# The low-query term of the attention logits, over 64 rows or over 128 with zeros

## The chip, the core and the metric

The kernel runs on one core of a Trainium2 chip. Its engines are TensorE (PE in the profile, with PEld for the loads of its stationary operand), VectorE (DVE), ScalarE (ACT), GpSimd (POOL) and SyncE (SP), whose queue issues the loads. The metric is the device time of one execution in microseconds, lower is better. Three runs of the kernel before took 865.79, 867.05 and 867.57 us; the median is 867.05.

## The reference

One layer of a hybrid decoder trunk over 512 tokens of width 1024, all in float32. A combined projection of the normalized input feeds three token mixers (a gated causal convolution, differential attention, causal pooling), whose outputs are gated, summed and projected; a squared-ReLU MLP and a gated embedding follow, each added to the residual. The change is in the attention, which has 4 heads with two softmax maps each over 64 dimensions:

```
q = q * (ATTN_HD ** -0.5)
for start in range(0, S, Q_BLOCK):                       # blocks of 128 queries
    qb, kb, vb = q[:, start:end], k[:, :end], v[:, :end]
    logits = jnp.einsum("bqhmd,bkhmd->bhmqk", qb, kb)    # m: the two maps, d: 64
    logits = jnp.where(dist >= 0, logits + bias, -1e30)
    probs = jax.nn.softmax(logits, axis=-1)
    attn = probs[:, :, 0] - lam * probs[:, :, 1]
    outs.append(jnp.einsum("bhqk,bkhe->bqhe", attn, vb))
```

## The kernel before

*Products in three terms.* A float32 operand is split into a rounded high part and the exact rest, both of a type (float32r) that TensorE multiplies quickly. A product is the sum of three matmuls, high with high, high with low and low with high; the helper at L153 to L155 issues them. Weights come in 144 chunks of 128 x 1024 through three raw slots; ScalarE rounds each chunk (L89) and VectorE subtracts (L93), into three pairs of slots (wh, wl).

*The order of work.* In its first half the kernel runs through the list ORDER: projections of conv, q and k, v and pool tiles, then gates and output products. Between the matmuls of these projections a clock of credit lets background streams (convolution, attention, pooling) issue their steps. The instructions are then ordered on each engine by the framework's scheduler, and each engine runs its own queue in that order. Heads 0 to 3 of the attention have their q and k projected at four places in the list, and `evac_qk` brings each out of PSUM.

*q and k of a head.* The 128 partitions of a projected tile hold the 64 dimensions of map 0 (LO) and of map 1 (HI). For each map m, `own` names its half and `other` the opposite one. Tile q[m] holds the high part of q twice, in both halves; k[m] holds the high part of k in `own` and the low part in `other`. One matmul of q[m] and k[m] over 128 rows (L460) is thus the sum of two terms, high q with high k and high q with low k. The third term, low q with high k, is a matmul over the 64 rows of `own` (L462). One tile `ql` serves both maps, each with its half. Both matmuls add into one PSUM bank.

*The logits.* For each head and each of 4 query blocks there are two maps, so 32 matmuls of L460 and 32 of L462, over 256, 256, 384 and 512 key columns. VectorE adds the bias and takes the maximum (L466), ScalarE does the exponential (L472), the two maps are combined, transposed on TensorE against an identity (L493), split, and multiplied by v. GpSimd clears the parts of the transposed tiles that stay zero (L498), issues the stores of an early projection (L364) and takes the powers of the norms (L202). The tiles q, ql and k come from one pool of 10 slots, five for a head.

Of the kernel before, what the change touches and what calls it, by code (L numbers as in the profile page):

```python
# [13 lines left out]

# the work of the first half in order, by the letters of the table
ORDER = [dict(A="conv", Q="qk", V="v", P="pool", p="pool out", a="attention out", c="conv gates")[c]
         for c in "QAVPAAQQQppppcAaaaaccc"]
# shares of TensorE's time given to the background work during projections and gates
RATE_IN, RATE_GATE = 0.6, 0.907
# of the steps of background work, how many are taken from the first queue for one from the second  # L20
TURNS = 2
# steps to wait for the sums of a norm: a head's, the last head's, LayerNorm's
NORM_LAG, WAIT_SUB, WAIT_LN = 10, 4, 8
# start: tiles of x loaded before the second chunk; chunks split before x is normalized; normalized
# tiles of x before the next chunks; products that bring up the array's clock
X_BEFORE_W1, W_EARLY, XN_BEFORE_W3, XN_BEFORE_W4, N_WARM = 3, 2, 2, 7, 8
# products of a half before the other half's sums, and before they are spread; chunks split after that
PACE_SUM, PACE_SPREAD, W_AHEAD = 8, 15, 3
# output tiles multiplied side by side before those by halves
N_SIDE = 3  # L30
# slots: raw chunks, split chunks, activations, logits, tiles of norms, q and k
N_RAW, N_SPLIT, N_ACT, N_LOGIT, N_NORM, N_QK = 3, 3, 32, 6, 3, 10
TCARGS = dict(schedule_with_timeline_sim=True)
# [11 lines left out]

# columns of the packed small parameters
G_PRE_MIX, G_POST_MIX, G_PRE_MLP, G_POST_MLP = 0, 8, 16, 24
# [9 lines left out]
class Weights:  # L57
    """Streams the packed weight chunks in order: a load and a split of each
    chunk into its rounded high part and the exact rest."""

# [50 lines left out]
def block_kernel(ctx: ExitStack, tc: tile.TileContext, xT, pT, wts, pool_w, par, rel_bias, onehot, out):  # L111
# [15 lines left out]

    # tiles that wait for a long chain have slots of their own: slots of a tag are
    # given out in order, so they would hold up all that comes after them
    BUFS = {"a": N_ACT, "lg": N_LOGIT, "bias": 2, "norm": N_NORM}  # L130
# [15 lines left out]
    def mul_split(h, l, src, scale=1.0):  # L146
        """h + l = src * scale, h rounded to the fast product's operand."""
        nc.scalar.activation(out=h, in_=src, func=AF.Copy, scale=scale)  # L148
        nc.vector.scalar_tensor_tensor(out=l, in0=src, scalar=scale, in1=h.bitcast(F32),  # L149
                                       op0=ALU.mult, op1=ALU.subtract)  # L150
# [5 lines left out]

# [1 line left out]
    start = ExitStack()  # L158
# [28 lines left out]
    nc.vector.memset(neghalf, -0.5)  # L187
    # products whose result nobody reads, so that the array's clock is up when the data comes
    warm = bank("at")
# [5 lines left out]

# [1 line left out]
    def rstd_from(ssq, inv_n, n, name):  # L197
        """[P, n] sums -> (sum * inv_n + eps) ** -0.5"""
        c = small(n, name + "c")
        nc.vector.tensor_scalar(out=c, in0=ssq, scalar1=inv_n, scalar2=EPS, op0=ALU.mult, op1=ALU.add)  # L200
        r = small(n, name + "r")
        nc.gpsimd.tensor_tensor(out=r, in0=c, in1=neghalf[:, 0:n], op=ALU.pow)  # L202
        return r

    def rstd_steps(sq, lo, n, inv_n, got, tag="at"):
        """column sums of sq[:, lo:lo+128n] to rstd, the same on every partition, in PSUM: a step
        for the sums and one that spreads them and hands them to got"""
        b = bank(tag)
        for j in range(n):
            nc.tensor.matmul(out=b[:, j:j + 1], lhsT=sq[:, lo + j * P:lo + (j + 1) * P], rhs=ones_col,  # L210
                             start=True, stop=True)
        r = rstd_from(b[:, 0:n], inv_n, n, "pe")
        yield
        for j in range(n):
            nc.tensor.matmul(out=b[:, j * P:(j + 1) * P], lhsT=r[:, j:j + 1].to_broadcast([P, P]),  # L215
                             rhs=ident, start=True, stop=True)
        got(b[:, 0:n * P])
# [16 lines left out]

    # ---- background streams: steps for DVE between the products, each step
    # yielding its cost in us, or None when it can't go on yet ----
    class Stream:
# [3 lines left out]
        def step(self):  # L241
            """one step; its cost, or None when the stream is blocked or over"""
            try:
                return next(self.gen)
            except StopIteration:
                self.over = True
                return None
# [41 lines left out]

# [1 line left out]
    LEFT, RIGHT = slice(0, 512), slice(512, 1024)  # L291
# [73 lines left out]

# [1 line left out]
    lam_t = cp.tile([P, 8], F32, name="lam_t")  # L367
# [11 lines left out]

    # sigmoid(z) = (1 + tanh(z / 2)) / 2, so that one table serves exp and the gates;  # L380
    # the factor 1/2 goes where a scale is applied anyway
    nc.vector.tensor_scalar(out=pcol(DW_W, 4 * CW), in0=pcol(DW_W, 4 * CW), scalar1=0.5, scalar2=None, op0=ALU.mult)
# [9 lines left out]
    nc.sync.dma_start(out=rel_d, in_=rel_r)  # L392
    # row r of a head's bias is its row of distances moved by r
    rep_d = dr.tile([NH, P, 640], F32, name="rep_d")
# [3 lines left out]

# [1 line left out]
    def project(n, evac, side_by_side=False):  # L400
        """n output tiles of the combined projection"""
        bs = []
# [17 lines left out]
    def evac_qk(bs):  # L420
        """q and k of a head's two maps, stacked so that a product over 128 rows holds two of the
        three terms: high q twice against high and low k; and low q where the high k lies"""
        qb, kb = bs
        ql = act_tile("ql", F32R, "qk", qkp)
        q, k = ([act_tile(n, F32R, "qk", qkp) for _ in range(2)] for n in "qk")
        for m, (own, other) in enumerate(((LO, HI), (HI, LO))):
            nc.scalar.activation(out=q[m][own], in_=qb[own], func=AF.Copy, scale=ATT_SCALE)
            nc.scalar.activation(out=q[m][other], in_=qb[own], func=AF.Copy, scale=ATT_SCALE)
            nc.vector.scalar_tensor_tensor(out=ql[own], in0=qb[own], scalar=ATT_SCALE, in1=q[m][own].bitcast(F32),
                                           op0=ALU.mult, op1=ALU.subtract)  # L430
            nc.scalar.copy(out=k[m][own], in_=kb[own])
            nc.vector.tensor_tensor(out=k[m][other], in0=kb[own], in1=k[m][own].bitcast(F32), op=ALU.subtract)
        return q, ql, k
# [15 lines left out]
    def attention():  # L449
        state = {}  # L450

        def logits(i):
# [6 lines left out]
            for m in range(2):  # L459
                nc.tensor.matmul(out=lg[m][:, 0:nn], lhsT=q[m][:, cols], rhs=k[m][:, 0:nn], start=True, stop=False)  # L460
            for m, own in enumerate((LO, HI)):
                nc.tensor.matmul(out=lg[m][:, 0:nn], lhsT=ql[own, cols], rhs=k[m][own, 0:nn], start=False, stop=True)  # L462
            mx, sm = small(2, "mx"), small(2, "sm")
# [23 lines left out]
        def transpose(i):  # L487
            # keys of all blocks up to this pair of query blocks on the partitions
            qb = i % 4
# [196 lines left out]

# [1 line left out]
    merged = [None] * KT  # L688
# [78 lines left out]

    # ---- output projection; its last tiles by token halves, so that the norm
    # of one half runs while the other half is multiplied ----
    x_t = []  # L770
# [13 lines left out]
    class Paced:  # L784
        """the steps of a norm, set between the products of the other half"""

# [14 lines left out]
    def split_output(src, evac, done):  # L801
        """8 output tiles of a product over 8 kt: some side by side, the others by halves."""
        W.limit = chunk[0] + KT + 3
# [38 lines left out]
    def residual_half(hf, src, ssum, rB, xs, use):  # L842
        """xs += src * rstd of the half, and what uses the sum"""
        sl = HALVES[hf]
# [18 lines left out]

# [1 line left out]
    def side_by_side_halves(src, done):  # L865
# [67 lines left out]

# [1 line left out]
    proj = []  # L935
# [36 lines left out]
def _layout(inp):  # L972
# [7 lines left out]
    def tiles(w):  # L980
        """[K, M] -> [M/128][128, K/128, 128]"""
        k, m = w.shape
        return w.reshape(k // P, P, m // P, P).transpose(2, 1, 0, 3)
# [88 lines left out]
```

## Time and profile before

| what | value |
|---|---|
| time, median of 3 runs | 867.05 us (865.79 to 867.57) |
| span of the profiled execution (no other time of it is given) | 864.5 us |
| TensorE matmul busy, instructions | 848.3 us (98%), 4202 |
| VectorE busy | 512.3 us (59%) |
| ScalarE busy | 352.5 us (41%) |
| GpSimd busy | 50.4 us (6%) |
| chain of work that ended last, share of TensorE | 86% |
| mean granted TensorE clock | 0.993 |

The span is the time from the first instruction to the last. Busy time of TensorE counts each matmul from its start to its modelled end, and one starts before the other has ended, so two matmuls in a row are compared by their starts. In a timeline row the numbers are the start, the time the row covers, the engine, the line, the operation, output and inputs by the program's names, rows*columns of the array that the operation uses, the shape it streams, and the count of instructions that the row merges; brackets give idle time ahead of it and what ended that.

### The profile page before, as it was taken

The numbers are of one execution on the slowest core, as the hardware profiler recorded it, in microseconds if no ns is written. First come the engines' busy times: TensorE is split into PE (matmuls) and PEld (weight loads), VectorE is DVE, ScalarE is ACT, GpSimd is POOL, SyncE is SP. The second block draws the span as 40 slices with busy tenths as digits, with TensorE's granted clock in tenths as the row PEclk, the third lists the DMA queues.
The fourth block names the chain that finished last, engine by engine and source line by source line (L and its number), as shares of the span: only waits on it lengthen the run. The fifth ranks groups of instructions, "written<-read, shape, count | busy, mean of one in ns | idle before, by whom it ended". The sixth has DMA issues, their size and how long they took to land.

```text
span 864.5 us, 10723 instructions
## 1 busy us (share of the span) xinstructions
PE 848.3 (98%) x4202; PEld 707.9 (82%) x4202; DVE 512.3 (59%) x803; ACT 352.5 (41%) x568; POOL 50.4 (6%) x85
## 2 busy tenths in 40 slices
PE   9979999999999999999999999999999999999998
PEld 6767888777778888888999778888888888889987
DVE  5749659965559996658368453344344434425682
ACT  6625435464443323553454354342124313425341
POOL 2100000010000000000033100000000000000420
PEclk9989999999999999999999999999999999999999
DMA  8353222121122222255201614222222222212311
GB/s 296 122 194 114 106 98 98 68 91 54 69 74 74 96 99 96 76 191 204 91 27 53 204 49 146 98 98 97 99 98 98 97 90 88 99 65 75 122 50 74
DMA packets 28127, 89.38 MB, mean 103 GB/s; under 512 B 3272, under 2 KB 3656, under 8 KB 28076
## 3 DMA queue, kind: packets, MB, share of 16 engines
q1 hardware_dynamic: 27260, 86.32, 28.6%
q0 software_dynamic: 816, 2.37, 0.7%
q8 instruction: 33, 0.54, 0.2%
q14 instruction: 18, 0.15, 0.1%
HBM read 84.47 MB, written 5.52 MB: 104 GB/s over the span
## 4 chain that ended last, share of the span: by engine, by line
PE 86%; DVE 5%; DMA 4%; issue 3%; ACT 1%; POOL 1%; SPq 0%; DVEq 0%; ACTq 0%; POOLq 0%
PE mm L153 19%; PE mm L155 19%; PE mm L154 19%; PE at L153 8%; PE at L154 8%; PE at L155 8%; DMA raw<-in_wts_dram 2%; DVE f L850 1%; PE at L462 1%; PE at L215 1%; POOL x L851 1%; PE at L210 1%; DVE mix L850 1%; PE at L460 1%; PE at L493 1%
## 5 line engine op out<-in xcount | busy, mean ns | idle before, releaser
L89 ACT CAST wh<-raw 128x1024 fp32r<-128x1024 f32 (+1 forms) x144 | 148.6, 1038 | 334.5 <-PE mm L154 151.0
L93 DVE TENSOR_TENSOR wl<-raw,wh 128x1024 fp32r<-128x1024 f32 (+1 forms) x144 | 173.4, 1209 | 104.6 <-ACT wh L89 104.3
L155 PE MATMUL mm<-xnh,wl 128*128 128x512 f32 x352 | 138.6, 394 | 0.1
L153 PE MATMUL mm<-xnh,wh 128*128 128x512 f32 x352 | 137.9, 394 | 0.0
L154 PE MATMUL mm<-xnl,wh 128*128 128x512 f32 x352 | 137.8, 392 | 0.0
L582 DVE SCALAR_TENSOR_TENSOR acc<-u,par_sb,acc 128x512 f32<-128x512 f32 x116 | 82.2, 748 | 0.1
L153 PEld LDWEIGHTS mm<-xnh,wh 128*128 128x128 f32 x352 | 66.1, 188 | 15.7 <-issue 1.0
L155 PEld LDWEIGHTS mm<-xnh,wl 128*128 128x128 f32 x352 | 66.1, 188 | 15.0 <-issue 0.8
L154 PEld LDWEIGHTS mm<-xnl,wh 128*128 128x128 f32 x352 | 66.1, 188 | 13.8 <-DVE xnl L149 0.4
L153 PE MATMUL mm<-sh,wh 128*128 128x512 f32 (+1 forms) x152 | 54.4, 358 | 0.0
L154 PE MATMUL mm<-sl,wh 128*128 128x512 f32 (+1 forms) x152 | 54.2, 357 | 0.0
L155 PE MATMUL mm<-sh,wl 128*128 128x512 f32 (+1 forms) x152 | 54.2, 356 | 0.0
L154 PE MATMUL at<-xgl,wh 128*128 128x512 f32 (+1 forms) x144 | 52.8, 366 | 1.2 <-DVE xgl L149 1.2
L153 PE MATMUL at<-sh,wh 128*128 128x512 f32 (+1 forms) x144 | 53.4, 371 | 0.3 <-ACT sh L148 0.3
L154 PE MATMUL at<-sl,wh 128*128 128x512 f32 (+1 forms) x144 | 53.1, 369 | 0.2 <-DVE sl L149 0.2
L155 PE MATMUL at<-sh,wl 128*128 128x512 f32 (+1 forms) x144 | 52.9, 367 | 0.0
L153 PE MATMUL at<-xgh,wh 128*128 128x512 f32 (+1 forms) x144 | 52.9, 367 | 0.0
L153 PE MATMUL mm<-xgh,wh 128*128 128x512 f32 (+1 forms) x144 | 52.7, 366 | 0.0
L155 PE MATMUL at<-xgh,wl 128*128 128x512 f32 (+1 forms) x144 | 52.7, 366 | 0.0
L154 PE MATMUL mm<-xgl,wh 128*128 128x512 f32 (+1 forms) x144 | 52.6, 365 | 0.0
L155 PE MATMUL mm<-xgh,wl 128*128 128x512 f32 (+1 forms) x144 | 52.6, 365 | 0.0
L202 POOL TENSOR_TENSOR per<-pec,neghalf 128x4 f32<-128x4 f32 (+1 forms) x10 | 10.5, 1052 | 533.2 <-DVE pec L200 533.2
(247 smaller groups left out, 1583.3 us busy)
## 6 DMA issues: line engine op xcount, KB each, us to landing
raw<-in_wts_dram SPq DMA_DIRECT2D x140, 512.0 KB, 3.2
x<-in_xT_dram SPq DMA_DIRECT2D x16, 256.0 KB, 5.9
proj_d<-proj POOLq DMA_DIRECT2D x8, 256.0 KB, 3.9
proj<-proj_d SPq DMA_DIRECT2D x8, 256.0 KB, 3.7
out_dram<-pg SPq DMA_DIRECT2D x7, 256.0 KB, 2.0
rep_d<-rel_d SPq DMA_DIRECT2D x1, 1280.0 KB
raw<-in_wts_dram SPq DMA_DIRECT2D x4, 256.0 KB, 5.4
bias<-rep_d SPq DMA_DIRECT2D x4, 256.0 KB, 4.5
```

What stands on the lines that cost most here:

```text
L89: i = self.nc.scalar.copy(out=wh[:, sl], in_=src)
L93: i = self.nc.vector.tensor_tensor(out=wl[:, sl], in0=src, in1=wh[:, sl].bitcast(F32), op=ALU.subtract)
L153: nc.tensor.matmul(out=o, lhsT=sh, rhs=mh, start=first, stop=False)
L154: nc.tensor.matmul(out=o, lhsT=sh, rhs=ml, start=False, stop=False)
L155: nc.tensor.matmul(out=o, lhsT=sl, rhs=mh, start=False, stop=last)
L202: nc.gpsimd.tensor_tensor(out=r, in0=c, in1=neghalf[:, 0:n], op=ALU.pow)
L210: nc.tensor.matmul(out=b[:, j:j + 1], lhsT=sq[:, lo + j * P:lo + (j + 1) * P], rhs=ones_col, start=True, stop=True)
L215: nc.tensor.matmul(out=b[:, j * P:(j + 1) * P], lhsT=r[:, j:j + 1].to_broadcast([P, P]), rhs=ident, start=True, stop=True)
L460: nc.tensor.matmul(out=lg[m][:, 0:nn], lhsT=q[m][:, cols], rhs=k[m][:, 0:nn], start=True, stop=False)
L462: nc.tensor.matmul(out=lg[m][:, 0:nn], lhsT=ql[own, cols], rhs=k[m][own, 0:nn], start=False, stop=True)
L582: nc.vector.scalar_tensor_tensor(out=t, in0=u[:, k:k + S], scalar=pcol(w0 + k), in1=t, op0=ALU.mult, op1=ALU.add)
L850: nc.vector.tensor_tensor(out=src[m][:, sl], in0=src[m][:, sl], in1=rB[:, sl], op=ALU.mult)
```

## The change

Map 0 and map 1 each get a tile `ql[m]` of 128 rows. Its `own` half takes the low part of q as before, its `other` half is cleared by GpSimd. The third term is then a matmul over all 128 rows, ql[m] with k[m]: in `own` low q meets high k, in `other` zeros meet low k. A head has six tiles in place of five, and the pool 12 slots in place of 10. The diff also takes out comments, and the lines move by three.

```
-N_RAW, N_SPLIT, N_ACT, N_LOGIT, N_NORM, N_QK = 3, 3, 32, 6, 3, 10
+N_RAW, N_SPLIT, N_ACT, N_LOGIT, N_NORM, N_QK = 3, 3, 32, 6, 3, 12
...
         qb, kb = bs
-        ql = act_tile("ql", F32R, "qk", qkp)
+        ql = [act_tile("ql", F32R, "qk", qkp) for _ in range(2)]
+        for m, other in enumerate((HI, LO)):
+            nc.gpsimd.memset(ql[m][other].bitcast(F32), 0.0)
...
-            nc.vector.scalar_tensor_tensor(out=ql[own], in0=qb[own], scalar=ATT_SCALE, in1=q[m][own].bitcast(F32),
+            nc.vector.scalar_tensor_tensor(out=ql[m][own], in0=qb[own], scalar=ATT_SCALE, in1=q[m][own].bitcast(F32),
...
-            for m, own in enumerate((LO, HI)):
-                nc.tensor.matmul(out=lg[m][:, 0:nn], lhsT=ql[own, cols], rhs=k[m][own, 0:nn], start=False, stop=True)
+            for m in range(2):
+                nc.tensor.matmul(out=lg[m][:, 0:nn], lhsT=ql[m][:, cols], rhs=k[m][:, 0:nn], start=False, stop=True)
```

On TensorE the first logits of head 0, with the first matmul of the next projection behind them, stand so in the kernel before:

```order
L460 MATMUL at_679<-k_418,q_416 128x256
L462 MATMUL at_679<-k_418,ql_415 128x256
L460 MATMUL at_680<-k_419,q_417 128x256
L462 MATMUL at_680<-k_419,ql_415 128x256
L460 MATMUL at_701<-k_418,q_416 128x256
L460 MATMUL at_702<-k_419,q_417 128x256
L462 MATMUL at_701<-k_418,ql_415 128x256
L462 MATMUL at_702<-k_419,ql_415 128x256
L153 MATMUL mm_443<-xnh_269,wh_386 128x512
```

and so in the changed kernel, where L463 is the old L460, L465 the old L462, and ql_415 and ql_416 are the tiles of the two maps:

```order
L463 MATMUL at_682<-k_421,q_419 128x256
L465 MATMUL at_682<-k_421,ql_415 128x256
L463 MATMUL at_683<-k_422,q_420 128x256
L465 MATMUL at_683<-k_422,ql_416 128x256
L463 MATMUL at_704<-k_421,q_419 128x256
L463 MATMUL at_705<-k_422,q_420 128x256
L465 MATMUL at_704<-k_421,ql_415 128x256
L465 MATMUL at_705<-k_422,ql_416 128x256
L153 MATMUL mm_446<-xnh_269,wh_386 128x512
```

Nothing moved here; each map's product reads a tile of its own. Lone products of the low part (the first two) and a pair side by side (the last two) stand where they stood, and so it is in the whole stream of TensorE, VectorE, ScalarE and the load queue.

On GpSimd the order does change. At the start of the program, where the identity for the transposes is made (masks.py), the kernel before has:

```order
masks.py:197 MEMSET ident 128x128
L498 MEMSET at_119_814 128x128
L498 MEMSET at_119_815 128x128
L498 MEMSET at_211_1340 128x128
masks.py:199 ISA
masks.py:199 AFFINE_SELECT ident<-ident 128x128
L498 MEMSET at_211_1341 128x128
L202 TENSOR_TENSOR per_239<-pec_237,neghalf 128x4
```

and the changed kernel:

```order
masks.py:197 MEMSET ident 128x128
L427 MEMSET ql_415 64x512
L427 MEMSET ql_416 64x512
L501 MEMSET at_120_817 128x128
masks.py:199 ISA
masks.py:199 AFFINE_SELECT ident<-ident 128x128
L501 MEMSET at_120_818 128x128
L501 MEMSET at_214_1349 128x128
L501 MEMSET at_214_1350 128x128
L202 TENSOR_TENSOR per_239<-pec_237,neghalf 128x4
```

The two memsets of head 0's low parts stand ahead of the identity's mask, and two of the transposed tiles' memsets have moved behind it.

Further on, behind the memset of the last conv tile but one (u) and with the zeros of the transposed maps (at) and the power of head 0's norm (per), the kernel before has on GpSimd:

```order
L567 MEMSET u_1088 128x30
L498 MEMSET at_244_1520 128x128
L498 MEMSET at_244_1521 128x128
L498 MEMSET at_274_1668 128x128
L498 MEMSET at_274_1669 128x128
L202 TENSOR_TENSOR per_1509<-pec_1507,neghalf 128x4
L498 MEMSET at_303_1814 128x128
L498 MEMSET at_303_1815 128x128
```

and the changed kernel, with the low parts of heads 2 and 3:

```order
L570 MEMSET u_1091 128x30
L427 MEMSET ql_1317 64x512
L427 MEMSET ql_1318 64x512
L501 MEMSET at_248_1532 128x128
L501 MEMSET at_248_1533 128x128
L501 MEMSET at_278_1680 128x128
L501 MEMSET at_278_1681 128x128
L202 TENSOR_TENSOR per_1521<-pec_1519,neghalf 128x4
L427 MEMSET ql_1454 64x512
L427 MEMSET ql_1455 64x512
L501 MEMSET at_307_1826 128x128
L501 MEMSET at_307_1827 128x128
```

Head 2's memsets come straight behind that of u, and head 3's behind the power; the others keep their order. Head 1's two stand further ahead, behind the stores of the early projection.

## Rows read from the trace of the kernel before

**Rows 1.** The page: its head, and busy time by engine.

```profile
span 864.5 us, 10723 instructions
...
PE 848.3 (98%) x4202; PEld 707.9 (82%) x4202; DVE 512.3 (59%) x803; ACT 352.5 (41%) x568; POOL 50.4 (6%) x85
```

**Rows 2.** TensorE's waits, whole span: total us, times, longest.

```profile
PE mm L153 <- ACT wh L89: 4.8, 1, 4.8
```

**Rows 3.** Busy time by stretch; the first line names the columns.

```profile
core 0: us, PE busy (x) PEld busy (x) DVE busy (x) ACT busy (x) POOL busy (x), PEclk, DMA share, GB/s
...
60.00:80.00 20.00, 20.00 (x87) 15.88 (x86) 20.00 (x44) 8.82 (x19) 0.00 (x0) 0.98 0.33 121
...
60.80:252.00 191.20, 191.20 (x880) 153.22 (x879) 140.07 (x286) 89.27 (x172) 6.26 (x16) 1.00 0.25 87
252.00:437.00 185.00, 185.00 (x912) 155.73 (x910) 130.47 (x178) 75.22 (x108) 2.52 (x3) 1.00 0.32 111
...
797.00:830.00 33.00, 29.99 (x239) 29.59 (x238) 25.18 (x46) 14.79 (x32) 15.43 (x18) 0.95 0.24 80
```

**Rows 4.** ScalarE's waits from 60 to 437 us: total us, times, longest.

```profile
ACT wh L89 <- PE mm L154: 70.6, 31, 5.3
```

**Rows 5.** Line L462 from 60 to 252 us: its matmuls, its idle time.

```profile
L462 PE MATMUL at<-k,ql x28: 379/437/502, 75.2 to 249.8; 64*128 64x256 f32 x12, 64*128 64x384 f32 x8, 64*128 64x512 f32 x8
...
  issue: 5.1, 19
```

**Rows 6.** Timeline of TensorE: the end of its longest wait.

```profile
56.27 2.07 PE L153 MATMUL mm<-wh,xnh 128*128 128x512 f32 x4 [4.83 <-ACT wh L89]
```

**Rows 7.** Timeline of TensorE: products over 128 rows in a run.

```profile
34.97 0.39 PE L153 MATMUL mm<-xnh,wh 128*128 128x512 f32 x1
35.20 0.39 PE L154 MATMUL mm<-xnl,wh 128*128 128x512 f32 x1
...
157.29 0.28 PE L154 MATMUL at<-at,vh 128*128 128x256 f32 x1
157.41 0.28 PE L155 MATMUL at<-at,vl 128*128 128x256 f32 x1
```

**Rows 8.** Timeline of TensorE: a lone product of the low part.

```profile
159.07 0.28 PE L460 MATMUL at<-k,q 128*128 128x256 f32 x1
159.28 0.38 PE L462 MATMUL at<-k,ql 64*128 64x256 f32 x1
159.59 0.50 PE L153 MATMUL mm<-xnh,wh 128*128 128x512 f32 x1
159.92 0.40 PE L154 MATMUL mm<-xnl,wh 128*128 128x512 f32 x1
```

**Rows 9.** Timeline of TensorE: two products of the low part side by side.

```profile
215.50 0.71 PE L460 MATMUL at<-k,q 128*128 128x512 f32 x2
216.14 0.50 PE L462 MATMUL at<-k,ql 64*128 64x512 f32 x2
216.58 0.50 PE L154 MATMUL mm<-xnl,wh 128*128 128x512 f32 x1
216.92 0.40 PE L155 MATMUL mm<-xnh,wl 128*128 128x512 f32 x1
```

**Rows 10.** Timeline of GpSimd: the mask, zeros, a power, a tensor operation.

```profile
1.40 0.29 POOL masks.py:199 TENSOR_SCALAR_AFFINE_SELECT ident<-ident 128x128 f32<-128x128 f32 x1
...
157.68 0.34 POOL L498 MEMSET at<- 128x128 f32 x2 [51.92 <-PE at L154]
...
181.50 1.96 POOL L202 TENSOR_TENSOR per<-pec,neghalf 128x4 f32<-128x4 f32 x1 [5.36 <-DVE pec L200]
...
441.50 6.97 POOL L851 TENSOR_TENSOR x<-x,mix 128x256 f32<-128x256 f32 x8 [3.07 <-PE at L155]
```

**Rows 11.** The chain of work: TensorE's first products against the identity.

```profile
18.05 1.05 PE at L215 x8
```

**Rows 12.** Timeline of TensorE: head 3's first product of the low part.

```profile
221.75 0.38 PE L462 MATMUL at<-k,ql 64*128 64x256 f32 x1
```

## The prediction

> **What bounds the kernel now.** I read the head of the page first: the span is 864.5 us and TensorE is busy for 98% of it, every other engine for 59% or less [rows 1]. Busy time alone does not make TensorE the bound, because matmuls overlap in the record, so the waits came next. TensorE's list of waits over the whole run has ten lines, and only the first is over 2 us: 4.8 us for a split weight chunk [rows 2]. The stretches show where it does not wait: from 60.8 to 437 us TensorE is busy in every microsecond (191.2 of 191.2, then 185.0 of 185.0) at a granted clock of 1.00, that is 2.4 GHz [rows 3]. The same can be read from the other side: ScalarE's split of the next chunk waits 70.6 us, in 31 places, for TensorE to give back the buffer [rows 4]. The feeders stand behind TensorE, so a microsecond taken from its stream there is a microsecond off the end.
>
> The changed line, L462, has 32 products. From 60 to 252 us lie 28 of them, 12 of 256 columns, 8 of 384 and 8 of 512 [rows 5]; the other four come before 40.3 us, ahead of the wait of 4.8 us, which ends at 56.27 [rows 6].
>
> **How the 64-row products are paid now.** A matmul's duration in the record is about its latency, so I read the distance from one start to the next. In a run of 128-row products the columns set it: 512 columns take 0.23 us (34.97 to 35.20), 256 columns 0.12 us (157.29 to 157.41) [rows 7]. Now a lone 64-row product among 128-row ones [rows 8]. L460 of 256 columns starts at 159.07 and the L462 behind it at 159.28, 0.21 where 0.12 is normal. The next product follows 0.31 later, where 0.12 is normal. That one's successor comes 0.33 later, at 159.92, where 0.23 is normal. The surplus is 0.09 + 0.19 + 0.10 = 0.38 us: the pipeline is not full once on the way into the 64-row form and once on the way out. The weight loads say the same, since those of L462 stand idle for 5.1 us in 19 places under "issue", the line's only wait [rows 5].
>
> Where two L462 stand side by side (the rows with x2, of which I count five in the timeline, the first at 39.95 and four after 60 us) the record is different. The pair of 512 columns at 216.14 takes 0.44 us until the next start, less than two normal products (0.46) [rows 9]: as far as the starts tell, the two halves of the array ran together there. So a pair has to be compared as a whole stretch: two L460 0.64 us (215.50 to 216.14), the pair 0.44, the product behind it 0.34.
>
> **The change part by part.** *The products.* Each L462 becomes a product of 128 rows by the same columns, the shape of L460, so I give it L460's normal distance and take away the surplus. Of the 28 from 60 us on, 28 less four pairs of two is 20 lone ones, and 20 x 0.38 is 7.6 us. I use the figure of 256 columns for all, because the surplus belongs to the way in and out and not to the columns; behind the pair of 512 columns the way out is the same (0.34 less 0.23). A pair: before 0.64 + 0.44 + 0.34 = 1.42, after 0.55 + 0.46 + 0.23 = 1.24, so 0.18 us, and 0.7 for four. Sum 8.3 us.
>
> The four early ones, two lone and a pair, would give 2 x 0.38 + 0.2, about 1.0 us. I count it as nothing: TensorE runs dry at 51.4 us and waits 4.83 until 56.27 for ScalarE's split of a chunk [rows 6], and finishing sooner makes that wait 5.8. I take that chunk to be late by its load and not by TensorE; if that cover were not there the sum would be 9.3.
>
> *The zeros.* Eight memsets of 64 x 512 on POOL are new. The trace has none of that shape. From below the nearest row is 0.34 us for two of 128 x 128, so 0.17; from above POOL's tensor operation on 128 x 256, 6.97 us for eight, doubled for 512 columns, 1.74 us [rows 10]. I take four times the memset, 0.7 us each. All of it is covered. The first two go ahead of the identity's mask, which ran at 1.40 us [rows 10] and is now later by 2 x 1.74 = 3.5 us at most; TensorE's first use of the identity is at 18.05 us [rows 11]. Those of the other heads stand earlier on POOL than their products do on TensorE. The tightest are the last two, behind the power that ends at 181.50 + 1.96 = 183.46 us [rows 10]: at 1.74 each they end at 186.9, and the first product that needs them starts at 221.75 [rows 12], 34.8 us later. So the new wait in the first products of three heads is met when TensorE gets there. What is queued behind these memsets on POOL are the zeros of the transposed maps, which ScalarE and VectorE then fill; those at 157.68 [rows 10] come behind head 2's memsets, which nothing but a memset of u long before holds up. If the cover failed, each late memset would hold all of TensorE's queue for as long as it is late.
>
> *The rest* is as it was: TensorE, VectorE, ScalarE and the load queue issue the same instructions in the same order. VectorE still writes 64 x 512 of q's low part, and two more slots take space and no time.
>
> **Against the runs.** The sum is made in an execution whose span is 864.5 us; that would become 856.2. The page gives no time for that execution beyond the span. The three runs have a median of 867.05, 2.55 above it. I take the 8.3 from the median: 858.8 us, 0.990 of before.
>
> **The rivals.** *The gap stays* (slower). The surplus belongs not to the row count but to something that L460 and L462 keep, such as going back and forth between q and its low part. Then the change removes nothing and takes away the overlap of the pairs: the second product of each pair pays a distance of its own. At normal distance that is at least 3 x 0.23 + 0.12 = 0.8 us for the four, and with the gap 4 x 0.44 = 1.8 at most: 867.9 to 868.8. The point that decides it is the start behind a lone product of 256 columns, 0.12 us on or 0.31. For it speaks that L462 is the only line with this pattern of operands. Against it: two L460 follow each other in 0.64 us, which is two normal distances with the way into L462 and a like step from the transpose ahead of them [rows 9], although they change operands too; and products that add into one bank follow each other at normal distance [rows 7]. The Trainium skill, "TensorE: Matmul & The Clock Gate", section "Why this matters for your kernels", has a rule that points the same way: one product over few rows takes the time of one over 128 rows, and the gain of the small form is that several run at once. By that rule alone the change could only lose. The pair of rows 9 agrees with it; the lone product of rows 8, 0.31 us against 0.12, does not come out of it, and 20 of the 28 are lone.
>
> *VectorE takes over.* It is busy for 20.00 of 20 us at 60 to 80 [rows 3]. If there and later half of what TensorE saves were given back in waits for VectorE, the time would be 867.05 - 4.1 = 862.9; if only what is saved in that first stretch (a pair and a lone one) were lost, 0.18 + 0.38 = 0.6 us, 859.4. Against it: TensorE waits for nothing in that stretch as it is, and VectorE has 191.2 - 140.1 = 51 us to spare from 60.8 to 252 [rows 3].
>
> *The clock.* The granted clock is 0.95 from 797 to 830 us [rows 3], so some 0.05 x 33 / 0.5 = 3.3 us of it at 1.2 GHz, costing at most 1.7 us. That stretch follows waits of the last norm. A dry spell at 51 us that is 1.0 us longer, and an end that comes 8.3 us sooner, may add such a stretch or drop this one: 860.5 or 857.1.
>
> **Chances and range.** The forecast with its own small errors (a surplus of 0.33 to 0.42 us per lone product, runs that differ by 1.8 us among themselves) has 0.76 and its range is 857.0 to 860.5. The clock has 0.10, VectorE 0.09, the gap that stays 0.05. What these runs can tell from no change is about 0.2%, 1.7 us. Only the gap that stays and the far end of VectorE's case come near that: same 0.04, slower 0.02, faster 0.94. The range takes in the first three cases, VectorE's nearly to half of the gain: 856.0 to 862.5.
>
> **What would show it.** In the profile after, every product of the low part should read 128*128, with the next start 0.12 us (256 columns) or 0.23 (512) behind it, and the product after that at 0.23 and not 0.33. The pairs should be the one place where products got dearer, 0.46 for two of 512 columns against 0.44. TensorE should still be busy in every microsecond from 61 to about 429 us, its wait that ends at 56 us should be about 5.8, and the memsets should have ended long before the products that read them. I am wrong if the distance behind a lone product stays at 0.31, if TensorE shows waits for VectorE or POOL between 60 and 430 us, or if the early chunk comes sooner when TensorE does, which would add up to 1.0 us to the gain.

## The result, and the profile after

| | before | after |
|---|---|---|
| median of the runs | 867.31 us (4) | 857.97 us (4; 857.13 to 858.45) |
| ratio, 95% interval | | 0.9896 (0.9880 to 0.9912), that is 7.6 to 10.4 us less |
| span of the profiled execution | 864.5 us | 856.7 us (its time 858.45) |
| span less the prediction's 8.3 | | 856.2 us |

The forecast was 858.8 us with a range of 856.0 to 862.5. The page after answers to [rows 1]: TensorE is still busy for 98%, with the same 4202 matmuls.

```profile
span 856.7 us, 10733 instructions
...
PE 839.4 (98%) x4202; PEld 709.4 (83%) x4202; DVE 511.6 (60%) x803; ACT 352.5 (41%) x568; POOL 54.6 (6%) x93
```

The stretches of the changed kernel, with the columns of [rows 3]: from 60.8 to 429 us TensorE is busy in every microsecond, as it was, so no new wait took the place of what was saved.

```profile
60.80:245.00 184.20, 184.20 (x887) 154.85 (x886) 140.81 (x290) 90.42 (x173) 8.45 (x20) 1.00 0.27 91
245.00:429.00 184.00, 184.00 (x910) 155.09 (x908) 129.46 (x177) 74.30 (x108) 2.52 (x3) 1.00 0.33 112
```

TensorE's timeline after, at the product that [rows 8] show before:

```profile
157.21 0.27 PE L463 MATMUL at<-k,q 128*128 128x256 f32 x1
157.32 0.28 PE L465 MATMUL at<-k,ql 128*128 128x256 f32 x1
157.44 0.40 PE L153 MATMUL mm<-xnh,wh 128*128 128x512 f32 x1
157.68 0.40 PE L154 MATMUL mm<-xnl,wh 128*128 128x512 f32 x1
```

The low part now reads 128*128. The starts are 0.11, 0.12 and 0.24 us apart, where they were 0.21, 0.31 and 0.33. The pair that [rows 9] show, after:

```profile
209.89 0.71 PE L463 MATMUL at<-k,q 128*128 128x512 f32 x2
210.44 0.63 PE L465 MATMUL at<-k,ql 128*128 128x512 f32 x2
210.91 0.39 PE L154 MATMUL mm<-xnl,wh 128*128 128x512 f32 x1
211.13 0.39 PE L155 MATMUL mm<-xnh,wl 128*128 128x512 f32 x1
```

Its two products take 0.47 us where they took 0.44 side by side, but the way in (0.55 for 0.64) and the way out (0.22 for 0.34) are shorter. The weight loads of the low part no longer stand idle: in [rows 5] they did for 5.1 us, and the same view of L465 has no idle time.

The early wait, after, answers to [rows 6]:

```profile
56.67 2.08 PE L153 MATMUL mm<-wh,xnh 128*128 128x512 f32 x4 [5.96 <-ACT wh L89]
```

It has grown from 4.83 to 5.96 us, by 1.13, and ends at 56.67 where it ended at 56.27. Of the 0.4 us between the two ends 0.3 was there before any logits: TensorE's product from which the relative bias is made (L389) starts 0.3 us later in this execution. Before and after:

```profile
20.41 1.02 PE L389 MATMUL at<-oh_sb,rb_sb 32*4 32x512 f32 x2
```

```profile
20.71 1.02 PE L389 MATMUL at<-oh_sb,rb_sb 32*4 32x512 f32 x2
```

From that product the wait ends 35.86 us later before and 35.96 after; it begins 31.03 us later before and 30.00 after. So TensorE comes 1.0 us sooner, and the chunk does not. The matmul behind the last logits, before and after, is

```profile
250.28 0.50 PE L155 MATMUL mm<-yh,wl 128*128 128x512 f32 x1
```

```profile
242.12 0.39 PE L155 MATMUL mm<-yh,wl 128*128 128x512 f32 x1
```

From the end of the wait to it TensorE needs 194.01 us before and 185.45 after, 8.56 less.

GpSimd's timeline, with the new memsets and what [rows 10] show:

```profile
1.00 1.10 POOL L427 MEMSET ql<- 64x512 f32 x2
...
2.29 0.28 POOL masks.py:199 TENSOR_SCALAR_AFFINE_SELECT ident<-ident 128x128 f32<-128x128 f32 x1
...
178.47 1.96 POOL L202 TENSOR_TENSOR per<-pec,neghalf 128x4 f32<-128x4 f32 x1 [5.37 <-DVE pec L200]
180.49 1.09 POOL L427 MEMSET ql<- 64x512 f32 x2
190.71 0.35 POOL L501 MEMSET at<- 128x128 f32 x2 [9.12 <-PE at L154]
```

A memset of 64 x 512 takes 0.55 us; the last pair is done at 181.6, 34 us before head 3's first product of the low part at 215.83.

### The profile page after: what moved, and what is told of

It is laid out like the page before. It is cut to its first block, busy times and chain, and to the rows that moved or that the text cites. A ratio compares the mean times of both kernels' runs of the same rounds, so it can differ in the third digit from the quotient of the medians.

```text
span 856.7 us, 10733 instructions
## 1 busy us (share of the span) xinstructions
PE 839.4 (98%) x4202; PEld 709.4 (83%) x4202; DVE 511.6 (60%) x803; ACT 352.5 (41%) x568; POOL 54.6 (6%) x93
## 4 chain that ended last, share of the span: by engine, by line
PE 86%; DVE 5%; DMA 4%; issue 3%; ACT 1%; POOL 1%; SPq 0%; DVEq 0%; ACTq 0%; POOLq 0%
PE mm L153 20%; PE mm L154 20%; PE mm L155 20%; PE at L153 8%; PE at L154 8%; PE at L155 8%; DMA raw<-in_wts_dram 2%; DVE f L853 1%; PE at L215 1%; POOL x L854 1%; PE at L210 1%; DVE mix L853 1%; PE at L465 1%; PE at L463 1%; PE at L496 1%
```

## The experiments

The theory: a 64-row product among 128-row ones costs TensorE a passage in and a passage out, that is, longer distances from start to start on the way into the other row count and back, about 0.4 us in all; the change takes 20 lone passages and four shared ones off an engine that is the bound; the zeros are free; the four early products earn nothing, because a weight chunk is late whatever TensorE does. The rivals are those of the prediction. The runs came in four groups, each with its own runs of the kernel before, whose medians were 866.6, 866.2, 867.0 and 866.7 us; the ratios below are against those of the same group. The times expected were counted from 867.3 and 858.0 us; the groups lay lower (the changed kernel, run again, by 1.2 us), and several medians lie just below their expected bounds for it, so the ratios and the differences within a group decide.

**Zeros without the rows (zeros_only).**

```
-                nc.tensor.matmul(out=lg[m][:, 0:nn], lhsT=ql[m][:, cols], rhs=k[m][:, 0:nn], ...)
+                nc.tensor.matmul(out=lg[m][:, 0:nn], lhsT=ql[m][own, cols], rhs=k[m][own, 0:nn], ...)
```

> The changed kernel with its two tiles, memsets and slots, but the low-query products again over the 64 rows of their own half (nothing is left out). Theory (each passage into and out of the 64-row form costs TensorE about 0.4 us in all, and zeros and slots cost nothing): the time of the kernel before, 867.3 us within 0.7; a lone product of 256 columns is again followed by a start 0.31 us later. Rival (the gain came with the separate tiles, slots or memsets, the row count is innocent): about 858.

866.3 us, ratio 0.9995 (0.9986 to 1.0005). TensorE's timeline shows the old distances beside the new tiles:

```profile
159.54 0.28 PE L463 MATMUL at<-k,q 128*128 128x256 f32 x1
159.75 0.38 PE L466 MATMUL at<-k,ql 64*128 64x256 f32 x1
160.06 0.50 PE L153 MATMUL mm<-xnh,wh 128*128 128x512 f32 x1
160.40 0.40 PE L154 MATMUL mm<-xnl,wh 128*128 128x512 f32 x1
```

Memsets, slots and separate tiles neither earn nor cost anything. What is left of the change is the row count.

**Only the four early products (early4).** The same line with `rows = slice(0, P) if i < 2 else own`.

> The changed kernel in which only the first four low-query products (head 0, query blocks 0 and 1, all ahead of TensorE's wait for a split chunk at 51 us) go over 128 rows; the other 28 stay over 64. Theory: TensorE saves 1.0 us there and waits 1.0 us longer, about 5.8 to 6.0 us until 56.3, so the time is that of before, 867.3 within 0.7. Rival (the chunk's load moves forward with TensorE): 866.3, wait still about 4.8.

866.96 us, ratio 1.0002 (0.9993 to 1.0010). The wait in its timeline:

```profile
58.31 2.08 PE L153 MATMUL mm<-wh,xnh 128*128 128x512 f32 x4 [5.99 <-ACT wh L89]
```

Ten profiles have this wait, and L389 starts between 20.4 and 22.3 us in them (latest in early4), so it is counted from there. With all early products over 64 rows it begins 31.0 us (before) and 31.1 us (zeros_only) later and lasts 4.83 us in both. With the early products over 128 rows it begins 30.0 us later in all six (after, after_again, early4, heads01, after_order, gates64) and lasts 5.74 to 6.07. In the two runs of pairs, described below, it begins 30.5 us later and lasts 5.51 and 5.20. In all ten it ends 35.7 to 36.1 us after L389: what is saved ahead of the wait is waited.

**Half a dose (heads01).** The same line with `rows = slice(0, P) if h < 2 else own`.

> Half a dose: heads 0 and 1 over 128 rows, heads 2 and 3 over 64. By the order these hold, after 60 us, 8 of the 20 lone products and 2 of the 4 pairs. Theory: 8 x 0.385 + 0.23 + 0.18 = 3.5 us less than before, 863.8 within 0.8. Rival (VectorE or the feeders give part of it back later, so that the first gains count less than the last): nearer 866; rival (the gain hangs on something that is there once): 867.3 or 858.

862.68 us, ratio 0.9955 (0.9942 to 0.9968), 2.8 to 5.0 us less, where 3.5 was forecast. The first half of the dose earns its part, so the gains are not given back later nor do they hang on one spot.

**A passage shared by two (pairs).** The kernel before, with

```
+            with tc.manual_schedule(engines={mybir.EngineType.PE}):
                 ...                     # the four matmuls of a query block
```

> The kernel before with its 64-row products, one ql tile and no memsets, but TensorE's four products of a query block kept in program order, so that all 32 stand as 16 pairs side by side (14 of them after 60 us). Theory: a passage is paid once for two products that run together; surplus over 128-row products 0.27 us for a pair of 256 columns, 0.23 for 384, 0.18 for 512, so 6 x 0.27 + 4 x 0.23 + 4 x 0.18 = 3.3 us is left of 8.4: 5.1 us less than before, 862.2 within 1. Rival (every 64-row product pays its own gap wherever it stands): 867.3 or more.

865.02 us, ratio 0.9980 (0.9972 to 0.9989): 1.0 to 2.4 us less, not 5.1. Here the theory missed, and the distances say that the passages were not what it missed. TensorE's timeline of a pair of 256 columns:

```profile
149.49 0.28 PE L461 MATMUL at<-k,q 128*128 128x256 f32 x1
149.70 0.39 PE L463 MATMUL at<-k,ql 64*128 64x256 f32 x2
150.02 0.50 PE L155 MATMUL mm<-xnh,wl 128*128 128x512 f32 x1
150.35 0.40 PE L153 MATMUL mm<-xnh,wh 128*128 128x512 f32 x1
```

Two products take the 0.32 us that a lone one took, with one way in (0.21) and one way out (0.33). In all 16 pairs the two start 3 to 4 ns apart, and the next start follows after 0.31 us for 256 columns, 0.37 for 384 and 0.42 to 0.43 for 512. Even so this pair with its ways in and out takes 0.27 us more than the same stretch of full products (0.86 against 0.12 + 0.24 + 0.23). But keeping four products together changed the order of other work on TensorE, VectorE and ScalarE, and TensorE's waits have a new line:

```profile
PE mm L153 <- ACT sg L570: 1.9, 1, 1.9
```

A matmul at 289.63 us waits there for a PSUM bank that ScalarE frees with the last conv gate. To take the order apart from the passages, the next two runs belong together.

**The order of pairs with 128 rows (after_order), and pairs once more (pairs_again).** The changed kernel with the same rule around its four matmuls.

> The changed kernel (128-row products with zeros) in the very order of the run pairs on TensorE, VectorE and ScalarE: a query block's four products kept in program order. It takes the order apart from the row count. Theory (the pairs saved 5.1 us of passages and lost about 3.5 again through the order that the rule brought with it, of which a wait of 1.9 us at 289.6 us is one part): 3.3 us less than pairs, 861.7 within 1.2, and 4 to 5 above the changed kernel in its own order. Rival (passages in pairs cost more than their distances show): the changed kernel's own 856.7 to 858.0, and 7 us or more below pairs.

> The run pairs once more, as the measure for the one before: 865.0 within 0.8, 3.3 us above it by the theory, 7 or more by its rival.

860.0 us (0.9933, 0.9917 to 0.9949) and 863.78 (0.9969, 0.9959 to 0.9979). The pairs stand 3.8 us above the same order with 128 rows, where 3.3 was forecast and the rival wanted 7. After_order has the same wait of 1.9 us for ScalarE, and it is 2.0 to 3.3 us slower than the changed kernel in its own order (857.97 and 856.73), less than the 4 to 5 that was said. So sharing a passage works about as the distances say, and the rule that brought it about spent 2 to 3 us on its order. That pairs itself came out at 0.9980 and then at 0.9969 shows how far two groups of runs of one kernel can lie apart.

**Passages where there is no attention (gates64).**

```
-            mm3(b, wh[:, kt * P:(kt + 1) * P], wl[:, kt * P:(kt + 1) * P], *xn[kt], kt == 0, kt == KT - 1)
...                                             # in its place, for kt == 0, the second of three products:
+                nc.tensor.matmul(out=b, lhsT=wl[LO, c], rhs=xn[0][0][LO], start=False, stop=False)
```

In each gate product one matmul, low weights with high x, goes over 64 rows in place of 128 and stands between the two others of its row block.

> The changed kernel, with one matmul in each of the 24 gate products (512 columns, no q, k or logits in it) turned from 128 into 64 rows and set between two matmuls of 128 rows: low weights times high x of the first of 8 row blocks, whose rows 64 to 127 are left out. As many matmuls as before, in nearly the same order. Theory (the surplus belongs to the passage between row counts, wherever it is): 24 x 0.40 = 9.6 us more than the changed kernel's 858.0, so 867.6 within 1; the start behind each is 0.42 us later and the next one 0.34. Rival (the surplus belongs to the operands of the logits, or was saved by the zeros): 858.0, starts 0.23 apart.

867.56 us, 10.8 above the 856.73 of after_again in the same group. TensorE's timeline shows one of the 24:

```profile
316.57 0.39 PE L699 MATMUL mm<-xnh,wh 128*128 128x512 f32 x1
316.89 0.50 PE L700 MATMUL mm<-xnh,wl 64*128 64x512 f32 x1
317.32 0.50 PE L701 MATMUL mm<-xnl,wh 128*128 128x512 f32 x1
317.65 0.39 PE L153 MATMUL mm<-xnh,wh 128*128 128x512 f32 x1
317.88 0.39 PE L154 MATMUL mm<-xnl,wh 128*128 128x512 f32 x1
```

The 64-row product starts 0.32 us behind the full one ahead of it, where 0.23 is normal; the starts behind it and behind its successor are 0.43 and 0.33 away, then 0.23 again. Summed over the 24 places, with the way in, the surplus in the trace is 9.68 us, 0.40 each; 9.6 was forecast. A product that has nothing to do with q, k or the logits pays the same: half the multiplications in these 24 matmuls made the kernel slower.

**The measure of that group (after_again).** The changed kernel once more.

> The changed kernel once more, as the measure for the others of this call. 858.0 within 0.7; its wait for the chunk at 50 to 57 us again about 5.9 us.

856.73 us, ratio 0.9891 (0.9870 to 0.9911), 1.2 us under what was expected; the wait is 5.74 us and ends at 56.97.

**Is it the chunk's load that hides the early four? (after_pool, before_pool)**

```
-    nc.sync.dma_start(out=rel_d, in_=rel_r)
+    nc.gpsimd.dma_start(out=rel_d, in_=rel_r)
...                                  # likewise the copy to rep_d and the load of head 0's bias
```

> The changed kernel with the two copies of the relative bias through DRAM and the first bias load issued from GpSimd's queue and not SyncE's. Theory (the early low-query products earn nothing because TensorE then waits for a weight chunk that stands behind the 1.25 MB copy of the bias in the load queue, and not for its own progress): the wait of 5.96 us falls below 1.5, the half clock after it shortens or goes, and the time is 4.5 to 7 us less than the changed kernel, 851 to 853.5. Rival (the chunk is late for another reason): 858.0.

> The kernel before with the bias copies and the first bias load on GpSimd's queue. Theory: the same 4.5 to 7 us come off, and with the wait gone the first four low-query products cost their 1.0 us again, so it stays 9.3 us above the changed kernel with the same move (8.3 without): 860.3 to 862.8. Rival (the first four are covered by something else too): 8.3 above it; rival (the two changes draw on the same time): less than 8 above it.

859.88 us (0.9928) and 869.61 (1.0040): both 3 us slower than without the move, so half of the theory fell. The wait at 50 to 57 us is gone, as forecast (TensorE is busy for 20.00 of 20 us from 40 to 60), but after_pool has a longer one in its place, and VectorE's waits from 50 to 70 us name the reason:

```profile
PE mm L154 <- DVE wl L93: 7.1, 1, 7.1
```

```profile
DVE lg L469 <- DMA bias<-rep_d: 12.3, 1, 12.3
```

VectorE stands for 12.3 us at the first logits, because the copy of the bias landed 20.3 us after its issue and head 0's bias came only then; the split of the next chunk is queued behind the logits on VectorE. Two things were late at the start, and I had known of one.

The distance between the two kernels is 9.7 us, near the 9.3 forecast, but it doesn't show that the early products count here. The new wait ends in after_pool and in before_pool at

```profile
68.12 0.80 PE L154 MATMUL mm<-wl,xnh 128*128 128x512 f32 x1 [7.13 <-DVE wl L93]
```

```profile
70.72 0.79 PE L154 MATMUL mm<-wl,xnh 128*128 128x512 f32 x1 [6.08 <-DVE wl L93]
```

and L389 starts at 19.88 and 22.49: the wait ends 48.2 us behind it in both, and is 1.05 us longer where the early products are shorter. They are waited away once more, and what else makes up the 9.7 stays open.

**Both waits at once (after_split, before_split).**

```
+    nc.sync.dma_start(out=rep_0, in_=...)      # head 0's quarter of the copy, ahead of the chunks
+    nc.gpsimd.dma_start(out=rep_d, in_=...)    # heads 1 to 3, and the load of head 1's bias
```

> The changed kernel with the copy of the relative bias cut in two: head 0's quarter stays in SyncE's queue ahead of the weight chunks, the other three heads' part and head 1's load go to GpSimd's queue. Theory (two waits bound the start: the chunk behind the whole copy, and, when the whole copy goes to GpSimd, head 0's bias on VectorE; a quarter in front is short enough for both): the wait of 5.7 to 6.0 us falls below 2 and none of over 2 us takes its place, 850 to 853.5. Rival (the copy through DRAM sets the pace in any queue): 856.7 to 860.

> The kernel before with the same cut. Theory (with the early wait gone TensorE is the bound from about 20 us on, so all 32 low-query products count, 8.5 us after 60 us and 0.9 before): 9.4 us above the changed kernel with the cut, 859.5 to 863. Rival (the first four stay hidden): 8.5 above it; rival (the early move and the row count draw on the same time): below 7.5 above it.

848.54 us (0.9787, 0.9769 to 0.9804) and 859.3 (0.9902, 0.9884 to 0.9920). The first is the fastest kernel of the study, 18.4 us under the one before. Its two stretches, and its longest wait, are:

```profile
38.00:60.00 22.00, 22.00 (x103) 18.32 (x102) 14.60 (x31) 9.92 (x19) 1.10 (x1) 1.00 0.54 184
60.00:430.00 370.00, 369.60 (x1834) 312.04 (x1833) 269.92 (x454) 166.85 (x281) 16.81 (x36) 1.00 0.31 102
```

```profile
PE at L210 <- DVE fsum L838: 1.8, 1, 1.8
```

TensorE no longer runs dry at the start and its clock stays at 1.00 there. One short wait in the stretch is new, for VectorE:

```profile
PE mm L153 <- DVE vl L149: 0.4, 1, 0.4
```

Between before_split and after_split lie 10.8 us by the medians, against 9.3 and 9.5 between after and before, and 9.4 were said; both kernels came out below their expected ranges. In the two traces L389 starts at 20.66 and 20.76, and the matmul behind the last logits reads, in before_split and after_split,

```profile
243.35 0.50 PE L155 MATMUL mm<-yh,wl 128*128 128x512 f32 x1
```

```profile
234.68 0.39 PE L155 MATMUL mm<-yh,wl 128*128 128x512 f32 x1
```

So TensorE gains 8.8 us in between, 9.2 without the new wait of 0.4. Of these 0.9 come at the four early products, which now count: the matmul behind them starts at 40.51 and 39.71. Some 1.7 more come later: in before_split's profiled execution the granted clock is 0.76 from 805 to 812 us, in that of after_split it is 1.00 at the same place of the program, 796 to 803 us.

## Why the prediction was right, step by step

*TensorE is the bound, and its waits tell.* Right. With 8.6 us taken out, the stretch from 60.8 to 429 us still has no wait. VectorE as the next bound is refuted by that and by the half dose; only in after_split, another 9 us faster, does a wait of 0.4 us for it appear there.

*The surplus of a lone product.* Right in kind and nearly in size: 0.38 us was taken for every width, read at 256 columns. Gates64 gives 0.40 for 512 columns. The sum from 60 us on was 8.3 and the trace has 8.56. The prediction's argument that the surplus belongs to the way in and out and not to the columns holds to 0.02 us.

*The pairs.* Right: 0.18 us each by comparing whole stretches, and after the change 0.55 + 0.47 + 0.22 = 1.24 as forecast. (Of the four pairs after 60 us three have 512 columns and one 384. The sum prices all as 512, and the rival of the gap that stays prices one as 256; either moves its sum by less than 0.1 us.) The rule of the Trainium skill that was weighed there ("TensorE: Matmul & The Clock Gate", "Why this matters for your kernels") describes the pair and not the lone product: gates64 shows a lone 64-row product at 0.40 us more than a 128-row one, not at the same.

*The gap that stays.* Refuted three times: by the 0.12 us behind the product of the low part after the change, by zeros_only, where the same tiles over 64 rows have the gap back, and by gates64, where the gap is made anew without q and its low part. What the engine does in a passage no run shows; the runs show what it costs and that it goes with the row count.

*The zeros.* Right that they are covered. The 0.7 us taken was too high; a memset takes 0.55, inside the bounds of 0.17 and 1.74.

*The four early products.* Right, and with the reason given: early4 measures no gain, TensorE reaches the wait 1.0 us sooner as was said, the wait's end stays where it was, and where no such wait is left (the split runs) the early products count for 0.9 us. What the prediction had not seen is that a second late transfer, head 0's bias, stands behind the first.

*From the trace to the runs.* The runs give 9.3 us and, in the second group, 9.45, the trace 7.8 from span to span and 8.56 in the stretch that matters. The interval of 7.6 to 10.4 holds all of these, so the 8.3 is not shown to be too small by the runs alone. What differs from execution to execution is the start (L389 starts between 19.9 and 22.5 us in the fourteen traces) and the clock after the last norm. These rows of after and of after_again, the same kernel, are stretches around it:

```profile
790.00:822.00 32.00, 29.26 (x232) 28.86 (x231) 24.59 (x45) 14.08 (x32) 15.45 (x18) 0.95 0.25 83
```

```profile
790.00:822.00 32.00, 28.98 (x242) 28.57 (x242) 26.31 (x46) 13.94 (x31) 14.87 (x18) 1.00 0.26 85
```

At a mean clock of 0.95 some 1.6 us are lost (0.05 x 32), at 1.00 none; the spans are 856.7 and 854.7. That is the clock rival of the prediction, seen as a scatter between executions.

How much of the 9.3 is clock can be estimated, because every run is on record with its span and its mean granted clock (to the nearest 0.001). Span times clock is about the time that the run would take at full clock; it also counts a slow clock as lost where TensorE only waits. For the 74 runs of the kernel before in the four groups the mean is 859.7 us, for the eight runs of the changed one 851.2, so 8.5 to 8.6 us of work, as the stretch in the trace has it. The other 0.7 of the 9.3 between their mean times goes with the clock, 0.9942 before and 0.9950 after. The same estimate puts gates64 9.8 us above after_again, where its distances sum to 9.68, and before_split 9.2 us above after_split, where 9.4 were said. So the forecast came near on its own term, 8.3 for 8.6, and left out 0.7 us of clock; whether the change brings that clock about or eight runs met it by chance is not shown.

## What to carry to other kernels

When TensorE is the bound, read distances from start to start and not durations, and look at what stands beside an instruction: a matmul of half the rows, alone among full ones, cost 0.4 us more than a full one with zeros. Side by side two of them shared the passage, but even so a pair cost 0.18 to 0.27 us more than two full ones; no run here has a group long enough to pay. Forcing them together took back, through the order of other work, about half of what the shared passages earned (2 to 3 of 5 us). And time saved ahead of a wait for a transfer is worth nothing until the wait goes; when it goes, ask what else was late behind it.

## What the runs showed of the hardware that was not expected

Two 64-row products on opposite halves of the partitions started 3 to 4 ns apart in all pairs and together took 0.31 us at 256 columns and 0.42 to 0.43 at 512 to the next start (pairs), but a lone one took just as long (0.31 in [rows 8], 0.42 to 0.43 in gates64). The whole copy of the bias, 1.25 MB from DRAM to DRAM in pieces of 2560 bytes, landed 20.3 us after its issue from GpSimd's queue in after_pool, about 65 GB/s, while weight chunks issued from SyncE's queue went through beside it.
